# Order of the mixing in a hybrid decoder layer: memory queries behind the memory keys, the values of dilated group 0 between the two dilated pairs, values read per head

## The chip, the cores and the metric

The kernel runs on one core of one Trainium2 chip. The metric is the device time of one execution in microseconds, the median over several runs. TensorE does the matrix products, VectorE (DVE) and ScalarE (ACT) the elementwise work, GpSimd (POOL) a few small operations and its own DMA queue, and SyncE (SP) issues most DMAs. Each engine and each queue takes its instructions in a fixed order.

## The reference

One decoder layer on 512 tokens of width 1024: a SwiGLU half-step, a token mixing, a second SwiGLU half-step, each between two RMS norms. The change lies in the mixing, which has three branches:

- HGRN2, a chunked gated linear recurrence with four heads;
- a dilated sliding-window attention: three groups (window 128, 512, 2048 with dilation 1, 4, 16) of four heads of width 128, each head with its own queries, keys and values. The groups of a head are merged by their softmax maxima and sums;
- a cross-attention of four heads into 256 memory tokens.

```
def token_mixing(u, mem, ...):
    proj = u @ w_in
    hq, hf, hi, hog, dcols, mq, gl = jnp.split(proj, SPLITS, axis=-1)
    y_hg = rmsnorm(hgrn2(hq, hf, hi, lb), hg_norm_w) * sigmoid(hog)
    y_dil = dilated_attention(dcols)
    y_mem = memory_attention(mq, mem, mem_norm_w, w_mem_kv)
    y = gate0 * (y_hg @ w_br_hg) + gate1 * (y_dil @ w_br_dil) + gate2 * (y_mem @ w_br_mem)
    return y @ w_out
```

## The kernel before, in words

All products are float32 made of three float32r products of high and low parts. A weight tile is loaded by SP into a staging buffer (`st`, `sh`, `sum`), its high part is made on ACT and its low part on DVE (`split`, line 160), and the parts go to a pool of 18 buffers named `w`. Two column blocks of 128 are made together by seven half-width products (`pair`, line 366; weight sums on DVE in `wops`, line 285); one such pair is 84 matmuls of 128x256. Values, which need tokens on the partitions, are made by plain products of 128x512 (`values`, line 847).

Order of the work. `mixing` (line 910) runs over the tuple ORDER (line 42): hg0 and hg1 are the two pairs of recurrence heads, prep and kv normalise the memory and make its keys and values, v0, v1, v2 make the values of the three dilated groups, dil0 and dil1 the queries, keys and scores of two dilated heads each, mq0 and mq1 the memory queries of two heads each; b_hg, b_mem and b_dil are gates and output products of the branches.

The long tails of each head are generators. They are put between the matmuls by a planner: every matmul adds its planned time to a clock (`tick`, line 109), and a generator that yields a number of microseconds (the table LAT, line 47) is taken up again when that much has been planned. A framework then places the instructions in the streams of the engines, and may put an instruction that it holds to be ready ahead of an earlier one; the order in each stream is fixed when the program is built. Weight loads run ahead of their use as far as staging buffers are free.

- `mem_attention` (line 570): scores of a head into PSUM (line 579), maximum (581), exponential (585), normalisation (589), transposes (595), product with the memory values (602), copy (604).
- `dil_scores` (line 721): scores of one group of a head, to `s0` (group 0) or `s12` (groups 1 and 2).
- `dil_values` (line 744): maxima (748), exponentials (759), the statistics of the two kinds of tile exchanged through DRAM by four DMAs of POOL (764 to 769), a wait of LAT dil1 = 17, factors and scaling (771 to 785), a wait of dil2 = 5, and then for `s0` and after it for `s12`: eight transposes (795; seven for `s0`), evictions to SBUF (798, 800), a wait of dil3 = 3, products with the values (812), and the result copied to y (814) or added to it (817).
- `put_values` (line 863) writes the values of a group to DRAM on ACT's queue; `get_values` (line 870) reads them for two heads in the token order of the group by two DMAs of SP, 256 KB each in runs of 1 KB. `dil_pair` (line 920) calls it once per group, right behind the scores of that group.

PSUM has three buffers `px` for the tails, SBUF 37 buffers `slot` for everything of 128x512.

Of the kernel before, what the change touches and what calls it, by code (L numbers as in the profile page):

```python
# [12 lines left out]
ALU = mybir.AluOpType  # L13
# [4 lines left out]
P = 128  # L18
# [20 lines left out]
NST = 4  # L39
HT = T // 2  # L40

ORDER = ("hg0", "prep", "v1", "hg1", "v2", "kv", "v0", "dil0", "mq0", "mq1", "dil1", "b_hg", "b_mem", "b_dil")

CHUNKS1 = (2, 4, 4, 4, 4, 4)
CHUNKS2 = (2, 4, 4, 4, 4, 4)
# [1 line left out]
LAT = dict(comb=1.0, mem0=0.5, mem1=8.0, mem2=1.5, hg=1.5, hgx=6.0, hg1=6.0, hg2=11.0, hg3=6.0, hg4=6.0, dil0=4.0, dil1=17.0, dil2=5.0,  # L47
           dil3=3.0, norm=8.0, mnorm=5.0, mload=10.0, start=0.1, step=2.0, keep=2.0)
# [4 lines left out]
class Layer:  # L53
# [687 lines left out]
            for i in range(2):  # L741
                self.tt(s[i][:, :, g - 1, :], sp[:, 2 * i:2 * i + 2, :], nb, ALU.add)

    def dil_values(self, hd, s0, s12, st0, st1, v, out):
        nc = self.nc
        hs = slice((hd % 2) * P, (hd % 2) * P + P)
        for i in range(2):
            nc.vector.tensor_reduce(out=st1[:, 2 * i:2 * i + 2, 0:1], in_=s12[i].rearrange("p a g b -> p a (g b)"), axis=AX.X, op=ALU.max)

        def block(s, i):  # L750
            b = s[i // 2][:, i % 2, :, :].rearrange("p a b -> p (a b)")
            return b[:, P:] if (s is s0 and i == 0) else b

        for s, st in ((s0, st0), (s12, st1)):
            nm = self.sm(4, "nm")
            nc.vector.tensor_scalar(out=nm, in0=st[:, :, 0], scalar1=-SCALE, scalar2=None, op0=ALU.mult)
            for i in range(4):
                b = block(s, i)
                nc.scalar.activation(b, b, AF.Exp, bias=nm[:, i:i + 1], scale=SCALE, accum_out=st[:, i, 1:2])


        x0 = self.dram.tile([T, 2], F32, tag=f"x0_{hd}", name=f"x0_{hd}")
        x1 = self.dram.tile([T, 2], F32, tag=f"x1_{hd}", name=f"x1_{hd}")
        nc.gpsimd.dma_start(out=x0.rearrange("(j p) c -> p j c", p=P), in_=st0)
        nc.gpsimd.dma_start(out=x1.rearrange("(p a) c -> p a c", a=4), in_=st1)
        ot0 = self.small.tile([P, 4, 2], F32, tag="ot0", name=f"ot0_{hd}")
        ot1 = self.small.tile([P, 4, 2], F32, tag="ot1", name=f"ot1_{hd}")
        nc.gpsimd.dma_start(out=ot0, in_=x1.rearrange("(j p) c -> p j c", p=P))
        nc.gpsimd.dma_start(out=ot1, in_=x0.rearrange("(p a) c -> p a c", a=4))
        yield LAT['dil1']  # L770
        for s, own, oth in ((s0, st0, ot0), (s12, st1, ot1)):
            mm, c = self.sm(4, "mm"), self.sm(4, "c")
            wt = self.small.tile([P, 2, 4], F32, tag="wt", name=f"wt{self.uid()}")
            self.tt(mm, own[:, :, 0], oth[:, :, 0], ALU.max)
            self.tt(wt[:, 0, :], own[:, :, 0], mm, ALU.subtract)
            self.tt(wt[:, 1, :], oth[:, :, 0], mm, ALU.subtract)
            nc.scalar.activation(wt, wt, AF.Exp, scale=SCALE)
            self.tt(mm, wt[:, 0, :], own[:, :, 1], ALU.mult)
            self.tt(c, wt[:, 1, :], oth[:, :, 1], ALU.mult)
            self.tt(mm, mm, c, ALU.add)  # L780
            nc.vector.reciprocal(mm, mm)
            self.tt(c, mm, wt[:, 0, :], ALU.mult)
            for i in range(4):
                b = block(s, i)
                nc.vector.tensor_scalar(out=b, in0=b, scalar1=c[:, i:i + 1], scalar2=None, op0=ALU.mult)
        yield LAT['dil2']

        y = self.slot()
        for s in (s0, s12):
            pTs = []  # L790
            for i in range(2):
                tp = self.paux((P, 4, P))
                lo = 1 if (s is s0 and i == 0) else 0
                for j in range(lo, 4):
                    self.transpose(tp[:, j, :], s[i][:, j // 2, j % 2, :])
                pT = self.slot((P, 4, P))
                if s is s0:
                    nc.scalar.copy(pT[:, lo:, :], tp[:, lo:, :])
                else:
                    nc.vector.tensor_copy(out=pT, in_=tp)  # L800
                pTs.append(pT)
            yield LAT['dil3']
            po = self.paux((P, 4, P))
            for b in range(4):
                pT, j = pTs[b // 2], 2 * (b % 2)
                if s is s0:
                    pairs = [(v[0][b - 1], pT[:, j, :])] if b > 0 else []
                    pairs.append((v[0][b], pT[:, j + 1, :]))
                else:
                    pairs = [(v[1][b], pT[:, j, :]), (v[2][b], pT[:, j + 1, :])]  # L810
                for n, (vv, pp) in enumerate(pairs):
                    self.mm(po[:, b, :], vv[:, hs], pp, n == 0, n == len(pairs) - 1)
            if s is s0:
                nc.scalar.copy(y, po.rearrange("p a b -> p (a b)"))
            else:
                yv = y.rearrange("p (s a) -> p s a", a=4)
                self.tt(yv, yv, po.rearrange("p a s -> p s a"), ALU.add)
        out[hd] = y


# [46 lines left out]
            self.nc.scalar.dma_start(out=d[t * P:(t + 1) * P, :], in_=v[t][:, 0, :])  # L867
        return d

    def get_values(self, d, g, hp):  # L870

        rows = d.rearrange("(p a) c -> p a c", a=4) if g else d.rearrange("(j p) c -> p j c", p=P)
        out = []
        for i in range(2):
            r = self.slot((P, 2, 256))
            self.nc.sync.dma_start(out=r, in_=rows[:, 2 * i:2 * i + 2, hp * 256:hp * 256 + 256])
            out += [r[:, j, :] for j in range(2)]
        return out

    def branch(self, b, y, w_in, w_br, z, last):  # L880

# [28 lines left out]
    def mixing(self, a, ready, nbias):  # L910
        nc = self.nc
        w_in = a["w_in"][0]
        y_hg, y_mem, y_dil = [None] * H, [None] * H, [None] * H
        t_hg, t_mem, t_dil = [], [], []
# [3 lines left out]
            t_hg.append(self.spawn(self.hgrn(hp, f, q, o, vh, y_hg)))  # L918

        def dil_pair(hp):  # L920
            heads, v = [], [None] * 3
            for i in range(2):
                hd = 2 * hp + i
                nb = self.slot()
                self.fetch(nb, nbias[:, hd, :])
                s0 = [self.slot((P, 2, 2, P)) for _ in range(2)]
                s12 = [self.slot((P, 2, 2, P)) for _ in range(2)]
                st0 = self.small.tile([P, 4, 2], F32, tag="st0", name=f"st0_{hd}")
                st1 = self.small.tile([P, 4, 2], F32, tag="st1", name=f"st1_{hd}")
                heads.append((hd, nb, s0, s12, st0, st1))  # L930
            scores = [[], []]
            pairs = self.pairs([(w_in, c, c + 512) for c in (C_DIL + g * 1536 + (2 * hp + i) * P for g in range(3) for i in range(2))])
            for g in range(3):
                for i, (hd, nb, s0, s12, st0, st1) in enumerate(heads):
                    if g == 0:
                        q, k = self.project2(next(pairs))
                    else:
                        q, k = self.slot((P, 4, P)), self.slot((P, 4, P))
                        perm = lambda x: x.rearrange("p (s a) -> p a s", a=4)
                        views = lambda x: [(x[:, :, h * 64:(h + 1) * 64], perm) for h in range(2)]  # L940
                        self.pair_out(self.pair(next(pairs)), views(q), views(k))
                    scores[i].append(self.spawn(self.dil_scores(nb, g, q, k, s0 if g == 0 else s12, st0)))
                v[g] = self.get_values(vd[g], g, hp)
            for i, (hd, nb, s0, s12, st0, st1) in enumerate(heads):
                self.need(*scores[i])
                t_dil.append(self.spawn(self.dil_values(hd, s0, s12, st0, st1, v, y_dil)))

        vh = [x[:, 0, :] for x in self.values(w_in, C_HI, 512, ready)]
        self.reset = self.slot()
# [2 lines left out]
        z, vd = None, {}  # L952
        for n, step in enumerate(ORDER):
            if step in ("hg0", "hg1"):
                hgrn_pair(int(step[2]))
            elif step in ("v0", "v1", "v2"):
                g = int(step[1])
# [3 lines left out]
            elif step == "prep":  # L961
                mT = [(self.slot((P, 2, NMEM), F32R), self.slot((P, 2, NMEM), F32R)) for _ in range(4)]
                prep = self.spawn(self.mem_prep(a["mem"][0], a["mem_norm_w"][0], mT))
# [3 lines left out]
            elif step in ("mq0", "mq1"):  # L967
                hp = int(step[2])
                mq = self.pairs([(w_in, C_MQ + hp * 2 * P, C_MQ + hp * 2 * P + P)])
                for i, q in enumerate(self.project2(next(mq))):  # L970
                    hd = 2 * hp + i
                    t_mem.append(self.spawn(self.mem_attention(hd, q, mkT[hd], mv, y_mem)))
            else:
                b, y, tasks, w = {"b_hg": (0, y_hg, t_hg, "w_br_hg"), "b_mem": (2, y_mem, t_mem, "w_br_mem"), "b_dil": (1, y_dil, t_dil, "w_br_dil")}[step]
                self.need(*tasks)
                z = self.branch(b, y, w_in, a[w][0], z, n == len(ORDER) - 1)
        return z
# [140 lines left out]
```

## Time and profile before

| what | us |
|---|---|
| median of 3 runs | 1367.01 |
| lowest and highest of them | 1365.49 and 1369.76 |
| the profiled execution | 1367.62 |
| its span, first to last instruction | 1365.8 |
| TensorE busy in that span | 1331.6 |

Granted TensorE clock, mean over the span: 0.998. A line of the profile names the source line (L158 is line 158), the engine, the operation, the tiles written and read (out<-in), the shapes and the count. L158 is the helper `tt` (any DVE operation of two tensors), L161 the high part of a split, L341 to L343 the products of 128x512, L361 to L363 those of a pair, L348 the small products of the tails, L352 a transpose, L151 a weight load. An idle time names what ended it. Ends of matmuls are modelled, so the starts are what is read.

### The profile page before, as it was taken

Reading aid. Unit: us, or ns where it says so; the run is one execution under the profiler, and the core shown is the slowest. Engines: PE = TensorE matmul, PEld = TensorE weight load, DVE = VectorE, ACT = ScalarE, POOL = GpSimd, SP = SyncE. Lnnn points to the kernel's source line nnn. Section 1 sums busy time; section 2 is a strip of 40 time slices with the busy share of each in tenths; the row PEclk is TensorE's granted clock in tenths of the full one; section 3 lists DMA queues with packets and bytes.
Section 4 is the critical chain, followed back from the end, with each engine's and each line's share of the span. In section 5 each row is a group of like instructions: output and inputs, shape, how many; then the busy total and the mean of one; then the engine's idle time right before and its main releaser. Section 6 shows DMA issues by size and latency. Waiting matters only on the chain.

```text
span 1365.8 us, 24324 instructions
## 1 busy us (share of the span) xinstructions
PE 1331.6 (97%) x9197; PEld 1233.0 (90%) x9197; DVE 1050.7 (77%) x1996; ACT 742.2 (54%) x1527; POOL 107.0 (8%) x140
## 2 busy tenths in 40 slices
PE   6999999999999999999999999999999999999997
PEld 6999999999789888899899999999889999999996
DVE  6887776777798975598888988897478877677765
ACT  6665544555467655355554755566366655445541
POOL 1111111110100000000000100000011111111100
PEclk9999999999999999999999999999999999999999
DMA  9676565554435335334224333335465765655513
GB/s 271 141 182 184 148 156 142 143 151 125 168 94 177 96 98 163 123 102 117 63 78 124 100 95 93 108 94 154 135 190 135 186 181 151 152 139 148 146 47 139
DMA packets 238123, 185.76 MB, mean 136 GB/s; under 512 B 9109, under 2 KB 198966, under 8 KB 238006
## 3 DMA queue, kind: packets, MB, share of 16 engines
q1 hardware_dynamic: 224246, 160.02, 39.5%
q0 software_dynamic: 12032, 21.04, 9.4%
q10 hardware_dynamic: 1728, 3.15, 0.6%
q8 instruction: 72, 1.18, 0.3%
q14 instruction: 45, 0.37, 0.1%
HBM read 153.73 MB, written 9.47 MB: 119 GB/s over the span
## 4 chain that ended last, share of the span: by engine, by line
PE 87%; DVE 6%; issue 3%; DMA 2%; ACT 1%; POOL 1%; SPq 0%; POOLq 0%; DVEq 0%; ACTq 0%
PE ps L361 17%; PE ps L363 17%; PE ps L362 17%; PE ps L341 6%; PE ps L342 6%; PE ps L343 6%; PE px L341 5%; PE px L342 5%; PE px L343 5%; PE px L348 4%; DVE s L158 2%; PE px L352 1%; DVE w L158 1%; POOL r L181 1%; DVE s L244 1%
## 5 line engine op out<-in xcount | busy, mean ns | idle before, releaser
L161 ACT ACTIVATE w<-sum 128x512 fp32r<-128x512 f32 x288 | 180.2, 631 | 215.9 <-PE ps L362 180.3
L158 DVE TENSOR_TENSOR w<-sum,w 128x512 fp32r<-128x512 f32 x288 | 196.9, 687 | 76.9 <-ACT w L161 75.9
L361 PE MATMUL ps<-xhi,w 128*128 128x256 f32 x864 | 246.3, 285 | 0.9 <-ACT s L379 0.9
L363 PE MATMUL ps<-xhi,w 128*128 128x256 f32 x864 | 244.8, 283 | 0.0
L362 PE MATMUL ps<-xlo,w 128*128 128x256 f32 x864 | 244.4, 283 | 0.0
L161 ACT ACTIVATE w<-st 128x512 fp32r<-128x512 f32 x260 | 162.9, 630 | 126.7 <-PE ps L362 90.0
L158 DVE TENSOR_TENSOR w<-st,w 128x512 fp32r<-128x512 f32 x260 | 177.2, 688 | 39.3 <-ACT w L161 37.9
L158 DVE TENSOR_TENSOR s<-s,s 128x256 f32<-128x256 f32 (+3 forms) x316 | 176.8, 564 | 16.2 <-ACT s L161 4.6
L361 PEld LDWEIGHTS ps<-xhi,w 128*128 128x128 f32 x864 | 165.6, 192 | 3.8 <-ACT s L379 1.2
L362 PEld LDWEIGHTS ps<-xlo,w 128*128 128x128 f32 x864 | 165.6, 192 | 2.4 <-issue 0.2
L363 PEld LDWEIGHTS ps<-xhi,w 128*128 128x128 f32 x864 | 165.5, 192 | 0.0
L158 DVE TENSOR_TENSOR sum<-sum,st 128x512 f32<-128x512 f32 x176 | 120.4, 687 | 10.9 <-issue 5.0
L158 DVE TENSOR_TENSOR s<-s,ps 128x256 f32<-128x256 f32 (+1 forms) x194 | 92.3, 476 | 29.4 <-PE ps L343 24.0
L341 PE MATMUL px<-s,s 128*128 128x512 f32 x288 | 112.6, 391 | 0.0
L342 PE MATMUL px<-s,s 128*128 128x512 f32 x288 | 112.5, 391 | 0.0
L343 PE MATMUL px<-s,s 128*128 128x512 f32 x288 | 112.0, 389 | 0.0
L361 PE MATMUL ps<-t4hi,w 128*128 128x256 f32 x288 | 81.9, 284 | 0.8 <-ACT s L382 0.8
L361 PE MATMUL ps<-t3hi,w 128*128 128x256 f32 x288 | 82.6, 287 | 0.0
L362 PE MATMUL ps<-t3lo,w 128*128 128x256 f32 x288 | 82.0, 285 | 0.0
L361 PE MATMUL ps<-t1hi,w 128*128 128x256 f32 x288 | 81.7, 284 | 0.0
L363 PE MATMUL ps<-t1hi,w 128*128 128x256 f32 x288 | 81.6, 283 | 0.0
L362 PE MATMUL ps<-t2lo,w 128*128 128x256 f32 x288 | 81.5, 283 | 0.0
(186 smaller groups left out, 3344.2 us busy)
## 6 DMA issues: line engine op xcount, KB each, us to landing
st<-in_ffn_w_gu_dram SPq DMA_DIRECT2D x48, 512.0 KB, 4.9
st<-in_w_in_dram SPq DMA_DIRECT2D x48, 512.0 KB, 3.7
st<-in_ffn_w_down_dram SPq DMA_DIRECT2D x44, 512.0 KB, 3.8
sum<-in_ffn_w_gu_dram SPq DMA_DIRECT2D x80, 256.0 KB, 3.4
sh<-in_ffn_w_gu_dram SPq DMA_DIRECT2D x40, 256.0 KB, 3.8
sum<-sh POOLq DMA_DIRECT2D x40, 256.0 KB, 3.6
sum<-st POOLq DMA_DIRECT2D x40, 256.0 KB, 3.3
sum<-in_w_in_dram SPq DMA_DIRECT2D x32, 256.0 KB, 2.9
```

What stands on the lines that cost most here:

```text
L158: self.pin(self.nc.vector.tensor_tensor(out=out, in0=a, in1=b, op=op))
L161: self.pin(self.nc.scalar.activation(hi, src, AF.Copy))
L181: self.nc.gpsimd.tensor_tensor(out=r, in0=v, in1=self.mhalf[:, :1], op=ALU.pow)
L244: self.nc.vector.scalar_tensor_tensor(out=h[hf][:, cs], in0=y[hf][:, cs], scalar=r, in1=h[hf][:, cs], op0=ALU.mult, op1=ALU.add)
L341: mm(out, lhsT=lhs[0], rhs=rhs[0], start=first, stop=False)
L342: mm(out, lhsT=lhs[0], rhs=rhs[1], start=False, stop=False)
L343: mm(out, lhsT=lhs[1], rhs=rhs[0], start=False, stop=last)
L348: self.nc.tensor.matmul(out, lhsT=lhsT, rhs=rhs, start=start, stop=stop, **k)
L352: self.nc.tensor.transpose(out, in_, self.ident)
L361: mm(out, lhsT=lh, rhs=rh, start=first and k == 0, stop=False, skip_group_check=True)
L362: mm(out, lhsT=lh, rhs=rl, start=False, stop=False, skip_group_check=True)
L363: mm(out, lhsT=ll, rhs=rh, start=False, stop=k == 3, skip_group_check=True)
```

## The change

ORDER is rewritten: kv, mq0 and mq1 follow hg1, then come v2, dil0, v0, dil1. `get_values` reads one head by one DMA of 256 KB in runs of 512 bytes, and is called in `dil_values` itself: for groups 1 and 2 when the head's transposes are due, for group 0 when `s12` is transposed and the values of group 0 exist. `s12` is done before `s0`; y is written by ACT from the product of `s12` and the product of `s0` is added by DVE.

```diff
--- before.py
+++ after.py
@@ -39,7 +39,7 @@
 NST = 4
 HT = T // 2
 
-ORDER = ("hg0", "prep", "v1", "hg1", "v2", "kv", "v0", "dil0", "mq0", "mq1", "dil1", "b_hg", "b_mem", "b_dil")
+ORDER = ("hg0", "prep", "v1", "hg1", "kv", "mq0", "mq1", "v2", "dil0", "v0", "dil1", "b_hg", "b_mem", "b_dil")
 
 CHUNKS1 = (2, 4, 4, 4, 4, 4)
 CHUNKS2 = (2, 4, 4, 4, 4, 4)
@@ -741,9 +741,9 @@
             for i in range(2):
                 self.tt(s[i][:, :, g - 1, :], sp[:, 2 * i:2 * i + 2, :], nb, ALU.add)
 
-    def dil_values(self, hd, s0, s12, st0, st1, v, out):
-        nc = self.nc
-        hs = slice((hd % 2) * P, (hd % 2) * P + P)
+    def dil_values(self, hd, s0, s12, st0, st1, vd, out):
+
+        nc = self.nc
         for i in range(2):
             nc.vector.tensor_reduce(out=st1[:, 2 * i:2 * i + 2, 0:1], in_=s12[i].rearrange("p a g b -> p a (g b)"), axis=AX.X, op=ALU.max)
 
@@ -786,7 +786,9 @@
         yield LAT['dil2']
 
         y = self.slot()
-        for s in (s0, s12):
+        yv = y.rearrange("p (s a) -> p s a", a=4)
+        v = {g: self.get_values(vd[g], g, hd) for g in (1, 2)}
+        for s in (s12, s0):
             pTs = []
             for i in range(2):
                 tp = self.paux((P, 4, P))
@@ -799,6 +801,10 @@
                 else:
                     nc.vector.tensor_copy(out=pT, in_=tp)
                 pTs.append(pT)
+            if s is s12:
+                while 0 not in vd:
+                    yield LAT['dil3']
+                v[0] = self.get_values(vd[0], 0, hd)
             yield LAT['dil3']
             po = self.paux((P, 4, P))
             for b in range(4):
@@ -809,12 +815,11 @@
                 else:
                     pairs = [(v[1][b], pT[:, j, :]), (v[2][b], pT[:, j + 1, :])]
                 for n, (vv, pp) in enumerate(pairs):
-                    self.mm(po[:, b, :], vv[:, hs], pp, n == 0, n == len(pairs) - 1)
+                    self.mm(po[:, b, :], vv, pp, n == 0, n == len(pairs) - 1)
             if s is s0:
-                nc.scalar.copy(y, po.rearrange("p a b -> p (a b)"))
+                self.tt(y, y, po.rearrange("p a b -> p (a b)"), ALU.add)
             else:
-                yv = y.rearrange("p (s a) -> p s a", a=4)
-                self.tt(yv, yv, po.rearrange("p a s -> p s a"), ALU.add)
+                nc.scalar.copy(yv, po.rearrange("p a s -> p s a"))
         out[hd] = y
 
 
@@ -867,15 +872,12 @@
             self.nc.scalar.dma_start(out=d[t * P:(t + 1) * P, :], in_=v[t][:, 0, :])
         return d
 
-    def get_values(self, d, g, hp):
+    def get_values(self, d, g, hd):
 
         rows = d.rearrange("(p a) c -> p a c", a=4) if g else d.rearrange("(j p) c -> p j c", p=P)
-        out = []
-        for i in range(2):
-            r = self.slot((P, 2, 256))
-            self.nc.sync.dma_start(out=r, in_=rows[:, 2 * i:2 * i + 2, hp * 256:hp * 256 + 256])
-            out += [r[:, j, :] for j in range(2)]
-        return out
+        r = self.slot((P, 4, P))
+        self.nc.sync.dma_start(out=r, in_=rows[:, :, hd * P:hd * P + P])
+        return [r[:, j, :] for j in range(4)]
 
     def branch(self, b, y, w_in, w_br, z, last):
 
@@ -918,7 +920,7 @@
             t_hg.append(self.spawn(self.hgrn(hp, f, q, o, vh, y_hg)))
 
         def dil_pair(hp):
-            heads, v = [], [None] * 3
+            heads = []
             for i in range(2):
                 hd = 2 * hp + i
                 nb = self.slot()
@@ -940,10 +942,9 @@
                         views = lambda x: [(x[:, :, h * 64:(h + 1) * 64], perm) for h in range(2)]
                         self.pair_out(self.pair(next(pairs)), views(q), views(k))
                     scores[i].append(self.spawn(self.dil_scores(nb, g, q, k, s0 if g == 0 else s12, st0)))
-                v[g] = self.get_values(vd[g], g, hp)
             for i, (hd, nb, s0, s12, st0, st1) in enumerate(heads):
                 self.need(*scores[i])
-                t_dil.append(self.spawn(self.dil_values(hd, s0, s12, st0, st1, v, y_dil)))
+                t_dil.append(self.spawn(self.dil_values(hd, s0, s12, st0, st1, vd, y_dil)))
 
         vh = [x[:, 0, :] for x in self.values(w_in, C_HI, 512, ready)]
         self.reset = self.slot()
```

## Rows read from the trace of the kernel before

**Rows 1.** The page, part 1: busy us, share and instructions of each engine.
```profile
PE 1331.6 (97%) x9197; PEld 1233.0 (90%) x9197; DVE 1050.7 (77%) x1996; ACT 742.2 (54%) x1527; POOL 107.0 (8%) x140
```

**Rows 2.** TensorE's waits, 380 to 870 us: waiter, releaser, total us, times, longest.
```profile
PE px L348 <- DVE s L158: 2.2, 3, 1.0
PE ps L342 <- DVE w L158: 1.8, 1, 1.8
PE px L348 <- ACT s L585: 1.6, 1, 1.6
PE px L352 <- DVE s L190: 1.0, 1, 1.0
PE ps L341 <- ACT w L161: 0.7, 1, 0.7
```

**Rows 3.** TensorE's timeline: start us, us, what, xcount, idle before and its releaser.
```profile
642.95 1.13 PE L348 MATMUL px<-s,s 128*128 128x128 f32 x8 [0.95 <-DVE s L158]
...
656.23 2.20 PE L348 MATMUL px<-s,s 128*128 128x256 f32 x8 [1.02 <-DVE s L158]
...
660.42 1.13 PE L348 MATMUL px<-s,s 128*128 128x256 f32 x4 [1.64 <-ACT s L585]
...
769.85 0.50 PE L341 MATMUL ps<-s,w 128*128 128x512 f32 x1 [0.72 <-ACT w L161]
```

**Rows 4.** Stretches: length; busy PE, PEld, DVE, ACT, POOL; clock; DMA share; GB/s.
```profile
517.00:546.00 29.00, 29.00 (x200) 25.55 (x199) 14.91 (x28) 13.16 (x24) 1.88 (x2) 1.00 0.54 172
546.00:574.00 28.00, 28.00 (x150) 22.59 (x149) 14.03 (x26) 8.12 (x14) 0.00 (x0) 1.00 0.35 108
...
633.00:653.00 20.00, 19.05 (x160) 18.88 (x159) 13.43 (x34) 11.80 (x38) 3.17 (x5) 1.00 0.30 81
653.00:686.00 33.00, 30.34 (x218) 26.50 (x217) 31.98 (x98) 17.50 (x47) 0.76 (x1) 1.00 0.20 57
686.00:746.00 60.00, 59.90 (x455) 56.44 (x454) 51.84 (x113) 32.27 (x78) 1.31 (x2) 1.00 0.40 106
```

**Rows 5.** Timeline of VectorE and of ScalarE behind dil0.
```profile
652.42 0.23 DVE L158 TENSOR_TENSOR mm<-st,ot 128x4 f32<-128x4 f32 x2 [4.76 <-DMA ot<-x]
...
659.35 0.47 ACT L585 ACTIVATE s<-px,mnm 128x256 f32<-128x256 f32 x1 [4.28 <-DVE mnm L582]
```

**Rows 6.** Memory attention on VectorE by line: ns min/median/max, first and last start.
```profile
L581 DVE TENSOR_REDUCE mmx<-px x8: 690/692/692, 658.3 to 691.3; 128x2 f32<-128x512 f32 x8
...
L589 DVE TENSOR_SCALAR s<-s,ml x16: 345/348/351, 662.2 to 696.1; 128x256 f32<-128x256 f32 x16
...
L604 DVE COPY s<-px x4: 684/688/694, 669.9 to 702.5; 128x512 f32<-128x512 f32 x4
```

**Rows 7.** Softmax exponentials of the dilated heads on ScalarE, line 759.
```profile
L759 ACT ACTIVATE s<-s,nm x32: 387/494/514, 593.0 to 768.2; 128x256 f32<-128x256 f32 x28, 128x128 f32<-128x128 f32 x4
```

**Rows 8.** Value reads, line 876: issues on SP, and issue to landing.
```profile
L876 SPq DMA_DIRECT2D s<-v x12: 408/460/1092, 596.0 to 757.7; - x12
...
DMA to landing us min/median/max: 3.8/5.7/7.5
```

**Rows 9.** Tile sh, 256 KB weight loads, issue to landing.
```profile
DMA to landing us min/median/max: 2.7/3.5/7.3
```

**Rows 10.** SP's waits, 560 to 800 us: waiter, releaser, total us, times, longest.
```profile
SPq L151 <- DVE w L158: 147.0, 33, 17.4
...
SPq L876 <- PE ps L362: 0.9, 2, 0.5
```

**Rows 11.** Eight transposes on TensorE, and two copies of the dilated heads by line.
```profile
676.16 1.04 PE L352 MATMUL px<-ident,s 128*128 128x128 f32 x8
...
L800 DVE COPY s<-px x8: 681/682/685, 677.2 to 796.8; 128x512 f32<-128x512 f32 x8
...
L814 ACT COPY s<-px x4: 586/586/587, 676.4 to 795.3; 128x512 f32<-128x512 f32 x4
```

**Rows 12.** Value writes, line 867 on ACT's queue: issue to landing.
```profile
DMA to landing us min/median/max: 2.0/2.0/2.7
```

## The prediction

> **What bounds the kernel now.** I read the share of each engine first: TensorE is busy for 1331.6 of 1365.8 us [rows 1], so the order of its work can only be worth the time in which it stands still. Next come its waits in the mixing [rows 2]. Leaving out 1.8 us, which precede the mixing, they make 2.2 + 1.6 + 1.0 + 0.7 = 5.5 us. This is the ceiling of what a new order can give back, 0.4% of the time. 0.3% is about what a measurement of this kernel can tell from no change, and is 4.1 us: below 1362.9 or above 1371.1.
>
> The timeline places the waits [rows 3]. At 642.95 the last scores of dil0 wait 0.95 us for the keys that DVE writes. At 656.23 and 660.42 the first scores of the memory queries wait 1.02 us for DVE, and 1.64 us until ACT's exponentials free a PSUM buffer. At 769.85 the first weight of b_hg comes 0.72 us late from ACT. The 1.0 us on L190 in [rows 2] belongs to the normalisation of the memory, which stays where it is; the remaining 0.20 us of the 2.2 is dil1's last scores.
>
> Why the memory queries wait is seen on the other engines. DVE has stood for 4.76 us before the statistics of the dilated heads, which come by DMA [rows 5], with everything else on its queue behind them. Then it owes two things at once, the dilated tails and the memory tails: from 653 to 686 us it is busy for 31.98 of 33.00 us [rows 4]. ACT, with the exponentials of the memory heads, waits 4.28 us for DVE's maxima [rows 5], and with that TensorE.
>
> **The change, part by part.** The sum starts from the profiled execution, 1367.62 us, which lies 0.61 above the median of the runs, 1367.01.
>
> *Memory queries behind kv.* Nothing is added: the same two pairs, scores, exponentials and transposes are issued earlier. Their DVE work is 8 maxima of 0.692, 16 scalings of 0.348 and 4 copies of 0.688 us [rows 6], together 5.5 + 5.6 + 2.8 = 13.9 us. It leaves a stretch where DVE had 1.02 us free and goes to one behind kv, where DVE is busy for 14.91 of 29.00 us, and under v2, which now follows (for v0, the same product, DVE is busy for 14.03 of 28.00) [rows 4]. The wait for the statistics is no longer ahead of it. Both waits should go: -1.02 - 1.64 = **-2.66 us**. The other bound is that they come back in the new place, where the tail of hg1 uses the same three PSUM buffers: 0. I take the whole gain, since DVE enters the new place without a backlog. The queries' weight loads pass those of v2, v0 and dil0 on SP's queue, and kv's follow hg1's directly; POOL's queue only loses distance to dil0's statistics. I cost that at 0: TensorE waits for no load in [rows 2], and loads run ahead. If that cover is gone, a late load costs TensorE up to its landing time, 3.5 us [rows 9].
>
> *v0 between the dilated pairs.* Its plain products now follow dil0, and need weights split on ACT and DVE while ACT has the exponentials of two heads, 16 of 0.494 us [rows 7], or 7.9 us. The nearest row is the end of dil1, where b_hg's plain products follow the same exponentials and TensorE waits 0.72 us for ACT [rows 3]. Bounds: 0, if the weights were split before, and 0.72. I take **+0.72 us**. The 4.76 us in which DVE waits for the statistics now fall into v0, whose 28 us need only 14.03 of DVE [rows 4]: 0. The writes of v0 stand behind the exponentials on ACT's queue, and land 2.0 us after their issue [rows 12]; who waits for them is the read of group 0, and behind that, on SP's queue, the weight loads of dil1. A read before waited 0.9 us in all on that queue [rows 10]; bounds 0 and 2.0, and I take 0, since loads run ahead of their use and TensorE waits for none in [rows 2]. The 0.95 us at dil0's end stays: the same scores are forced out at the end of the pair, behind the same keys.
>
> *Values read per head when due.* The count stays 12 reads of 256 KB, each taking some 0.46 us of SP to issue [rows 8], in runs half as long. Their place changes: before, they were issued behind each group's scores and landed long before use; now they are issued when the transposes are due. Between issue and use lie eight transposes, which end 1.04 us after their start, and the planned 3 us of other products, so 4.0 us, with two evictions of 0.682 us beside them [rows 11]. A read took 3.8 to 7.5 us to land, 5.7 in the median [rows 8]. Weight loads of the same size, whose runs are 128 columns or 512 bytes as the new reads' are, landed in 3.5 us [rows 9]. So a head waits between 0 and 7.5 - 4.0 = 3.5 us; four heads, 0 to 14.0. I take **0**, the value of the loads with the same shape.
>
> The trace so shows no penalty for runs of 512 bytes against 1 KB: 3.5 us against 5.7 [rows 8, 9]. The Trainium skill, Perfetto Trace Analysis, section DMA Optimizations, speaks against this part: it has small DMAs, under 2 KB, carry significant overhead each, and would batch them. If halving the run doubled the landing to an estimated 11.4 us, the four heads would wait 4 x 7.4 us, and the time would be near 1395. The rows do not bear that out.
>
> *The swap of `s12` and `s0`.* ACT still makes four copies, of 0.586 us [rows 11], DVE four additions; the reordered write is now ACT's. Cost 0, far off TensorE's path; if the copy became slow it would hold a PSUM buffer a little longer. The buffers in SBUF are less used, since the values of a pair no longer wait through its scores: no cost, and no wait for one shows today beyond the 0.9 us.
>
> Sum: 1367.62 - 2.66 + 0.72 = 1365.68 for an execution like the profiled one, and with 0.61 off, **1365.1** as a median.
>
> **The rivals.**
>
> *A, the forecast*, chance 0.45: 1365.1, its own range 1363.4 to 1367.0 (with v0's weights on time 1364.4).
>
> *B, the wait only moves*, 0.13. The order in the tuple is not that of the streams, and hg1's tail takes PSUM and DVE as the dilated tails did. The 2.66 us stay and 0.72 is added: 1367.7. Against it: both new stretches have some 14 us of DVE free [rows 4].
>
> *C, the other waits go too*, 0.20. v0's products, ready early, fill the wait at dil0's end, and the relief of DVE reaches dil1's: 1367.01 - 2.66 - 0.95 - 0.72 - 0.20 = 1362.5. For it: those are DVE and ACT waits [rows 3]; against: the keys are forced out as before.
>
> *D, TensorE waits for the values*, 0.22, the slower one. TensorE takes its stream in order, so a product placed too soon after its read holds all pairs behind it. At the median landing each head is short by 5.7 - 4.0 = 1.7 us; four heads give 6.8, and 1371.9. At 7.5 us it is 14.0, and 1379.1. It decides from 6.0 us in all, 1.5 per head. For it: SP is mostly waiting, 147.0 us of 240 for buffers that DVE frees, up to 17.4 at once [rows 10], and a read placed behind such a load is late with it. Against: two heads run together and share a wait, and the framework may put pair products ahead. The Trainium skill's rule on small DMAs, cited above, would raise this price to 4 x 7.4 us; as the rows stand I leave it 0.02 of the 0.22.
>
> **How the numbers follow.** The likeliest is A, 1365.1. Faster by over 0.3% is nearly all of C: 0.20. Slower is D with a little of B: 0.23. A and B make the rest, 0.57. The range runs from 1361.8, a little below C, to 1372.5, which takes in D at the median landing; D's upper part and a luckier C are left out, less than 2 in 10.
>
> **What would show it.** Right: TensorE's waits name neither L585 nor a memory score, DVE between kv and v2 is busier than [rows 4] but not full, and a wait on ACT stands at v0's first product. D shows as small products idle until a DMA of the value tiles. B shows as the same wait on L585 near 530 us. If TensorE's idle time grows in dil1's first pair by DVE's weight splits, the transition v0 to dil1 was costed too low, and the prediction is wrong there.

## The result, and the profile after

The changed kernel is slower: 1372.58 us median (13 runs, 1369.45 to 1376.12) against 1367.85 for the kernel before (13 runs on the same chip, 1365.36 to 1369.76), ratio 1.0031 with a 95% interval of 1.0020 to 1.0043. The forecast, 1365.1, has the wrong sign, and the median lies 0.08 us above the end of the range. The profiled execution took 1375.53 us, span 1373.8.

Part 1 of its page, busy time by engine, answers to [rows 1]:

```profile
PE 1337.2 (97%) x9197; PEld 1239.0 (90%) x9197; DVE 1049.6 (76%) x1996; ACT 742.3 (54%) x1527; POOL 106.7 (8%) x140
```

The count of TensorE's instructions is the same, 9197, and yet it is busy for 5.6 us more. Its waits from 380 to 870 us, to be read against [rows 2]:

```profile
PE px L348 <- DMA s<-v: 3.1, 1, 3.1
PE px L348 <- DVE st L734: 2.2, 2, 1.9
PE ps L342 <- DVE w L158: 1.8, 1, 1.8
PE px L352 <- DVE s L190: 1.0, 1, 1.0
PE ps L341 <- ACT w L161: 0.7, 1, 0.7
PE px L348 <- DVE s L158: 0.7, 2, 0.5
```

The wait of 1.64 us on the exponentials, L585, is gone, and that on L158 fell from 2.2 to 0.7 us: the memory queries no longer hold TensorE. Two waits are new, one on DVE's masking of scores (L734) and one on a read of values. TensorE's timeline places them, and the wait of b_hg that stood at 769.85 in [rows 3]:

```profile
610.83 0.70 PE L348 MATMUL px<-s,s 128*128 128x256 f32 x2 [1.88 <-DVE st L734]
...
695.05 0.77 PE L348 MATMUL px<-s,s 128*128 128x128 f32 x2 [3.10 <-DMA s<-v]
...
777.70 0.50 PE L341 MATMUL ps<-s,w 128*128 128x512 f32 x1 [0.72 <-ACT w L161]
```

The first stands at the first scores of dil0, the second in the first pair of dil1. Stretches behind the two, with the columns of [rows 4] (length; busy PE, PEld, DVE, ACT, POOL; clock; DMA share; GB/s):

```profile
608.00:611.00 3.00, 1.12 (x6) 0.67 (x6) 2.97 (x8) 1.23 (x3) 0.00 (x0) 1.00 0.31 87
611.00:614.00 3.00, 3.00 (x17) 2.95 (x18) 2.44 (x10) 1.01 (x3) 0.00 (x0) 0.64 0.50 126
614.00:617.00 3.00, 3.00 (x22) 3.00 (x22) 2.12 (x5) 2.21 (x9) 0.00 (x0) 0.80 0.15 54
...
692.00:694.00 2.00, 0.00 (x0) 0.00 (x0) 1.89 (x4) 0.00 (x0) 0.00 (x0) 0.93 1.10 331
694.00:697.00 3.00, 1.95 (x9) 1.98 (x10) 0.41 (x1) 0.00 (x0) 0.00 (x0) 0.50 0.57 163
697.00:700.00 3.00, 3.00 (x16) 3.00 (x16) 1.57 (x3) 0.09 (x1) 0.00 (x0) 0.50 1.02 287
700.00:703.00 3.00, 3.00 (x27) 3.00 (x26) 0.00 (x0) 1.98 (x4) 0.00 (x0) 0.91 0.09 28
```

The eighth column is the one that matters. Behind each wait the granted clock falls, to 0.50, which is 1.2 of 2.4 GHz (behind the first it is 0.50 from 612 to 615 us, within the two stretches shown); in [rows 4] it is 1.00 in every stretch. While TensorE works at that clock it loses, by length times what is missing from 1.00, 3.00 x 0.36 + 3.00 x 0.20 = 1.7 us behind the first wait, and from 695.05 to 703 us 4.95 x 0.50 + 3.00 x 0.09 = 2.7 us behind the second. So in this execution the wait of 1.88 costs 3.6 us, and that of 3.10 costs 5.8.

That accounts for this execution. What left: 1.02 + 1.64 of the queries, and 0.4 of the 0.95 at dil0's end (the wait on L158 has now 0.5 as its longest), 3.1 us. What came: 3.6 + 5.8 = 9.4. The balance is +6.3 us. By the timelines, from the first product of hg0 to the first of b_hg, the kernel before took 769.85 - 398.07 = 371.8 us and this one 777.70 - 399.77 = 377.9: +6.1. The rest of the 7.9 us between the two profiled executions lies ahead of the mixing, where the change is not (a clock of 0.52 from 383 to 386 us, behind a wait of 1.8 us that both kernels have); it comes and goes between executions.

These prices hold for the profiled execution, which is the second longest of the 13. Its mean granted clock is 0.994. That of the three longest, 1375.35 to 1376.12 us, is 0.993 or 0.994; that of the other ten, 1369.45 to 1373.20 us, is 0.995 to 0.998, and the kernel before had 0.998 in its profiled execution. So most executions seem to pay less for the clock than this one, and the medians are only 4.7 us apart. How the 4.7 us divide between waits and clock is not shown.

**Why the values came late.** SP's timeline, its issues around 690 us:

```profile
683.07 0.37 SPq L151 DMA_DIRECT2D sum<-in_w_in_dram  x1
685.60 0.37 SPq L151 DMA_DIRECT2D st<-in_w_in_dram  x1
686.06 1.01 SPq L141 DMA_DIRECT2D s<-in_nbias_dram  x2
687.12 1.33 SPq L879 DMA_DIRECT2D s<-v  x2
688.54 0.62 SPq L151 DMA_DIRECT2D sh<-in_w_in_dram  x1
694.37 2.30 SPq L879 DMA_DIRECT2D s<-v  x4
```

SP's waits from 660 to 700 us (as [rows 10]), and the landing time of the two reads issued at 687.12 (as [rows 8]):

```profile
SPq L151 <- DVE w L158: 27.4, 4, 13.8
SPq L879 <- DMA v<-s: 5.0, 1, 5.0
```

```profile
DMA to landing us min/median/max: 7.8/7.9/7.9
```

One weight load had held SP for 13.8 us, until DVE had split earlier weights. Then dil1's weights, two masks (L141), the reads of groups 1 and 2 and v0's last write all fell within 6 us, and the DMA engines moved 331 GB/s from 692 to 694 us. The reads took 7.8 us to land; TensorE was ready for them at 695.05 - 3.10 = 691.95, 4.8 us after their issue. 7.8 - 4.8 = 3.0 is the wait. Four more reads follow from 694.37. The first of them is a read of group 0, which held SP's queue for 5.0 us until v0's last write had landed; ACT had issued that write at 687.25, into the same burst, and it took 7 us.

**Why dil0 starts late.** DVE's timeline before the first scores:

```profile
588.87 2.00 DVE L158 TENSOR_TENSOR w<-sum,w 128x512 fp32r<-128x512 f32 x3 [0.46 <-ACT w L161]
...
600.86 0.69 DVE L158 TENSOR_TENSOR sum<-sum,sh 128x512 f32<-128x512 f32 x1 [2.51 <-issue]
```

The weight sum at 600.86 waits 2.51 us. The view names nobody for that wait ("issue"), but the semaphore events of the same trace do: it ends with the landing, at 600.78, of a load to `sh`. SP's issues around it:

```profile
592.10 0.37 SPq L151 DMA_DIRECT2D st<-in_w_in_dram  x1
592.56 1.01 SPq L141 DMA_DIRECT2D s<-in_nbias_dram  x2
594.51 0.38 SPq L151 DMA_DIRECT2D sh<-in_w_in_dram  x1
```

The load was issued at 594.51, behind another weight load and two masks, and landed 6.3 us later. It is a burst like that at v0's end, without the value reads. DVE then has no free time until the scores ask for it (2.97 of 3.00 us busy from 608 to 611), and they wait for L734.

### The profile page after: what moved, and what is told of

Same layout as the page of the kernel before. It is cut to its first block, busy times and chain, and to the rows that moved or that the text cites. A ratio compares the mean times of both kernels' runs of the same rounds, so it can differ in the third digit from the quotient of the medians.

```text
span 1373.8 us, 24321 instructions
## 1 busy us (share of the span) xinstructions
PE 1337.2 (97%) x9197; PEld 1239.0 (90%) x9197; DVE 1049.6 (76%) x1996; ACT 742.3 (54%) x1527; POOL 106.7 (8%) x140
## 4 chain that ended last, share of the span: by engine, by line
PE 84%; DVE 6%; issue 3%; DMA 3%; ACT 2%; POOL 1%; SPq 0%; DVEq 0%; POOLq 0%; ACTq 0%
PE ps L361 16%; PE ps L363 16%; PE ps L362 16%; PE ps L341 6%; PE ps L342 6%; PE ps L343 5%; PE px L341 5%; PE px L342 5%; PE px L343 5%; PE px L348 5%; DVE s L158 2%; PE px L352 1%; DVE w L158 1%; POOL r L181 1%; DVE s L244 1%
## 5 line engine op out<-in xcount | busy, mean ns | idle before, releaser
L158 DVE TENSOR_TENSOR w<-sum,w 128x512 fp32r<-128x512 f32 x288 | 196.7, 688 | 77.2 <-ACT w L161 76.2
L158 DVE TENSOR_TENSOR w<-st,w 128x512 fp32r<-128x512 f32 x260 | 178.0, 689 | 38.9 <-ACT w L161 31.8
L158 DVE TENSOR_TENSOR s<-s,s 128x256 f32<-128x256 f32 (+3 forms) x316 | 177.2, 565 | 16.0 <-ACT s L161 4.6
L158 DVE TENSOR_TENSOR sum<-sum,st 128x512 f32<-128x512 f32 x176 | 120.4, 688 | 13.8 <-issue 7.2
L158 DVE TENSOR_TENSOR s<-s,ps 128x256 f32<-128x256 f32 (+1 forms) x194 | 92.5, 477 | 29.2 <-PE ps L343 24.0
L363 PE MATMUL ps<-t1hi,w 128*128 128x256 f32 x288 | 82.2, 286 | 0.0
L362 PE MATMUL ps<-t1lo,w 128*128 128x256 f32 x288 | 81.9, 284 | 0.0
L361 PE MATMUL ps<-t2hi,w 128*128 128x256 f32 x288 | 81.8, 284 | 0.0
```

Source lines behind the costliest of these rows:

```text
L158: self.pin(self.nc.vector.tensor_tensor(out=out, in0=a, in1=b, op=op))
L361: mm(out, lhsT=lh, rhs=rh, start=first and k == 0, stop=False, skip_group_check=True)
L362: mm(out, lhsT=lh, rhs=rl, start=False, stop=False, skip_group_check=True)
L363: mm(out, lhsT=ll, rhs=rh, start=False, stop=k == 3, skip_group_check=True)
```

## The experiments

Theory: the queries' move is a gain, and what outweighs it is two late transfers (reads of values at v0's end, weights behind v2), each of which costs the wait and, in some executions, a fall of the clock behind it. Rivals: the late reads are slow in themselves; moving the queries is what costs; v0 between the pairs costs whatever the reads do. Each run stands against the kernel before on the same chip (medians 1367.00 in the first four runs, 1367.13 in the next four, 1367.26 in the last four).

### The parts alone

**e1_queries_only**: the kernel before, with the queries behind kv, and v2 and v0 ahead of dil0.

```diff
-ORDER = (..., "hg1", "v2", "kv", "v0", "dil0", "mq0", "mq1", "dil1", ...)
+ORDER = (..., "hg1", "kv", "mq0", "mq1", "v2", "v0", "dil0", "dil1", ...)
```

> The kernel before with kv, mq0 and mq1 behind hg1 and v2, v0, dil0, dil1 after them; the value reads stay as they were. Theory (three separate effects: the moved queries gain about 4 us, the late reads lose about 6, the start of dil0 behind v2 loses about 4): 1363 to 1365 us, no wait on L585, and dil0's first scores wait no longer than the 0.4 us they wait in the kernel before, since dil0 follows v0 as it did. Rival (the moved memory tails crowd VectorE and that is what delays dil0's first scores): the wait of 1.9 us on L734 comes back and the time is 1367 to 1369.

Measured: 1365.49 us, ratio 0.9987 (0.9977 to 0.9997). The wait on L585 is gone. The move is a gain of some 1.5 us, not a cost. It is less than the 2.66 that went; two small waits are new in its trace, 0.6 on L734 and 0.7 on L604 (DVE's copy of the product with the memory values). The time is 0.5 us above the theory's range, and well below the rival's.

**e2_reads_only**: the changed kernel in the order of the kernel before.

```diff
-ORDER = (..., "kv", "mq0", "mq1", "v2", "dil0", "v0", "dil1", ...)
+ORDER = (..., "v2", "kv", "v0", "dil0", "mq0", "mq1", "dil1", ...)
```

> The changed kernel with the order of before: only the late reads per head and the swap of s12 and s0 are left. Theory (the reads are late because SP was held and then sent a burst of weight loads, bias loads and reads at the end of v0): in the old order dil0's reads stand among the loads of mq0, without that burst; TensorE waits at most 1 us per pair for values and the time is 1367 to 1369. Rival (a read issued when due is late anywhere): a wait of 3 us and a fallen clock at each pair, 1373 to 1379.

Measured: 1365.50 us, 0.9991 (0.9982 to 0.9999). No wait names the values; the 1.6 us on L585 stay. Reads of one head in 512-byte runs, issued when due, cost nothing in themselves, nor does the swap of `s12` and `s0`. The time lies below the 1367 to 1369 of the theory.

**e4_v0_ahead**: the changed kernel with v0 back ahead of dil0.

```diff
-ORDER = (..., "v2", "dil0", "v0", "dil1", ...)
+ORDER = (..., "v2", "v0", "dil0", "dil1", ...)
```

> The changed kernel with v0 ahead of dil0 again, so that dil1 follows dil0 directly; late reads per head stay. Theory: no plain product stands between the pairs, SP isn't held by its weight buffers, and the reads wait for no write; the wait on s<-v falls to under 1 us: 1365 to 1368. Rival (the tails of dil0 need a light stretch of VectorE, which v0 gave): TensorE waits in dil1's first pair for weights or scores by 3 us or more, 1370 to 1373.

Measured: 1365.76 us, 0.9996 (0.9984 to 1.0007); no wait on a read, 0.7 us on L734. So each part is harmless without v0 between the pairs. With v0 there the reads are late, and the kernel is 0.3% slower, dil0's late start included.

### The reads of values in dil1's first pair

**e3_reads_early**: the reads of groups 1 and 2 at the start of the values of a head, 22 us of planned work earlier.

```diff
     def dil_values(self, hd, s0, s12, st0, st1, vd, out):
+        v = {g: self.get_values(vd[g], g, hd) for g in (1, 2)}
...
-        v = {g: self.get_values(vd[g], g, hd) for g in (1, 2)}
```

> The changed kernel with the reads of groups 1 and 2 issued at the start of dil_values, ahead of the softmax, some 22 us earlier. Theory (late reads cause the wait of 3.1 us at dil1's start, and the wait makes the clock fall): no wait on s<-v for these groups, granted clock 1.00 there, 1366 to 1368. Rival (the traffic at the end of v0 itself holds TensorE, through weights and the read of group 0): the wait moves to another tile and the time stays at 1371 to 1373.

Measured: 1368.25 us, 1.0013 (1.0001 to 1.0024). TensorE's waits from 380 to 870 us:

```profile
PE px L348 <- DVE st L734: 2.2, 2, 1.8
PE px L352 <- DVE s L190: 1.0, 1, 1.0
PE px L348 <- DVE s L158: 0.8, 2, 0.6
PE px L348 <- ACT s L800: 0.7, 1, 0.7
```

These are the four largest; the fifth is b_hg's 0.7. The wait for the values is gone, and with it the low clock: 1.00 from 691 to 700 us. In its place stand 0.7 us on ACT's copy of transposes (L800). At dil0's start all stays as it was (1.8 us on L734, a clock of 0.53 behind it).

**e10_reads_on_pool**: the reads on POOL's queue, past SP's held load.

```diff
-        self.nc.sync.dma_start(out=r, in_=rows[:, :, hd * P:hd * P + P])
+        self.nc.gpsimd.dma_start(out=r, in_=rows[:, :, hd * P:hd * P + P])
```

> The changed kernel with the value reads issued on GpSimd's queue instead of SP's. Theory (SP was held from 669 to 683 us by one weight load and the reads of groups 1 and 2 stood behind it and behind the bias loads): on the other queue they are issued earlier, some ms of the burst no longer precede them, and the wait for values falls to 1 us or less, 1366 to 1369. Rival (the reads are placed late by the plan, at the transposes): they leave at the same time and the wait stays above 2 us, 1371 to 1374.

Measured: 1376.47 us, 1.0076 (1.0055 to 1.0097), the slowest of all. POOL's timeline, and the wait that comes of it on TensorE's:

```profile
670.69 1.49 POOL L879 DMA_DIRECT2D s<-v  x2
691.22 2.99 POOL L879 DMA_DIRECT2D s<-v  x4 [19.03 <-DMA sum<-in_w_in_dram]
```

```profile
695.60 0.46 PE L348 MATMUL px<-s,s 128*128 128x128 f32 x2 [4.37 <-DMA s<-v]
```

Two reads now start 16 us earlier, and nobody waits for that head. But the other four stand 19 us on the queue and are issued only at 691.22. By the program the first of the four is group 0's, which needs v0's last write. The view names another DMA, but the semaphore events of the trace bear the program out: the queue went on at 690.54, when the last update of that write's semaphore had come at 690.52. ACT had issued the write at 684.11. The reads of groups 1 and 2 of the other head are among the four, and TensorE waits for them, longer than before; 1.9 us on DVE's copies (L802) are new as well. Neither the theory (1366 to 1369) nor the rival (1371 to 1374) foresaw the time. The Trainium skill, Perfetto Trace Analysis, section DMA Optimizations, suggests balancing DMAs across the engines that can issue them, where generating descriptors is the bottleneck. It was not the bottleneck here, where an issue takes SP some 0.6 us and one load had held it for 13.8, and the trace shows the other side: a queue of its own keeps its order too, and one read that is not ready holds all those behind it.

### dil0's start

**e8_bias_early**: all four mask biases are loaded at the start of kv, so that the bursts behind v2 and v0 are 512 KB smaller.

```diff
-                nb = self.slot()
-                self.fetch(nb, nbias[:, hd, :])
+                nb = nbs[hd]
...
             elif step == "kv":
                 self.need(prep)
+                for hd in range(H):
+                    nbs.append(self.slot())
+                    self.fetch(nbs[hd], nbias[:, hd, :])
```

> The changed kernel with the four bias loads of 256 KB (nbias) sent at the start of kv instead of at the head of each dilated pair, where two of them leave SP between the weight loads and the value reads. Theory (bursts: where a dilated pair follows plain products, SP is held by a weight buffer and then sends weights, biases and reads within 3 us, so that each lands late): dil0's wait on L734 falls from 1.9 to under 1 us, the wait for values at dil1's start from 3.1 to 1.5 us or less, the clock stays at 1.00 at one of the two places at least: 1366 to 1369. Rival (the reads and weights are late because they leave late, not because of what is ahead of them): both waits stay within 0.5 us, 1371 to 1373.

Measured: 1369.50 us, 1.0021 (1.0008 to 1.0034). DVE's wait before the weight sum fell from 2.51 to 1.26 us (the load to `sh` now lands in 5.0 us). Of TensorE's waits these bear on the theory:

```profile
PE px L348 <- DVE s L802: 2.1, 1, 2.1
...
PE px L348 <- DVE st L734: 0.6, 1, 0.6
PE px L348 <- DMA s<-v: 0.6, 1, 0.6
```

The clock stays 1.00 from 605 to 617 us. In dil1's first pair the reads land earlier, and what is late next is DVE's copy of the transposes (L802): 2.1 + 0.6 us instead of 3.1. The clock is 0.54 from 691 to 694 us. The time is 0.5 us above the theory's range.

**e9_v0_ahead_bias_early**: e8 with v0 ahead of dil0, as in e4.

> The changed kernel with v0 ahead of dil0 and the bias loads early. Theory (bursts): dil0's wait on L734, 0.7 us with v0 ahead alone, falls to the 0.03 us that it is in the kernel before; nothing else changes: 1363 to 1365, ratio to before 0.997 to 0.999. Rival (no burst effect there): the wait stays, the time is that of v0 ahead alone.

Measured: 1365.42 us, 0.9991 (0.9980 to 1.0002). The wait on L734 that e4 has is gone, but 1.7 us on L802 are new, behind b_hg's first product. The time is 0.4 us above the theory's range, and against e4 it is no difference that can be told.

**e6_dil0_behind_mq**: the changed kernel with v2 ahead of kv, so that dil0 follows the memory queries, which are pairs, and not a plain product.

```diff
-ORDER = (..., "hg1", "kv", "mq0", "mq1", "v2", "dil0", "v0", "dil1", ...)
+ORDER = (..., "hg1", "v2", "kv", "mq0", "mq1", "dil0", "v0", "dil1", ...)
```

> The changed kernel with the order hg0, prep, v1, hg1, v2, kv, mq0, mq1, dil0, v0, dil1: dil0 now follows a pair, not plain products; v0 stays between the dilated pairs. Theory (two separate costs, one at each place where a dilated pair follows plain products): the wait on L734 at dil0's start falls to 0.4 us or less and the clock stays at 1.00 there; the wait for values of some 3 us at dil1's start stays with its fall of the clock: 1368 to 1371. Rival (the memory tails crowd VectorE in dil0): they now run in dil0 itself, waits of 2 us or more in dil0 and 1372 or more.

Measured: 1371.00 us, 1.0030 (1.0018 to 1.0042). The wait on L734 is gone and the clock is 1.00 there; the wait for the values is still 2.7 us, with a clock of 0.72 from 691 to 697. The two losses are separate. The second alone is, in this profiled execution, 2.7 us of waiting and 6.00 x 0.28 = 1.7 us of clock, 4.4 in all; the next run takes it away from here.

### Both losses taken away, and v0 in other company

**e7_dil0_behind_mq_early**: e6 with the early reads of e3.

> The changed kernel with both of its losses taken away by order and place alone: v2 ahead of kv, so that dil0 follows the memory queries and not a plain product (run e6 showed no wait of 1.9 us at dil0's start that way), and the reads of groups 1 and 2 issued at the start of the values of a head (run e3 showed no wait for them that way). v0 stays between the dilated pairs. Theory (the loss is those two waits and the clock behind them, not v0's place as such): TensorE names neither s<-v nor L734 above 0.7 us, the granted clock is 1.00 from 600 to 760 us, and the time is 1365 to 1367. Rival 1 (v0 between the pairs costs by itself, whatever the reads): a wait of 1 us or more at dil1's start on DVE or ACT, and 1368 to 1370. Rival 2 (the reads of group 0, which must wait for v0's last write, become the wait): s<-v of 1 to 3 us near 690 us and 1369 to 1371.

Measured: 1366.11 us, 0.9996 (0.9987 to 1.0005), some 5 us under e6, whose ratio is 1.0030. All of TensorE's waits from 380 to 870 us:

```profile
PE ps L342 <- DVE w L158: 1.8, 1, 1.8
PE px L352 <- DVE s L190: 1.0, 1, 1.0
PE px L348 <- ACT s L585: 0.8, 2, 0.5
PE ps L341 <- ACT w L161: 0.7, 1, 0.7
PE px L348 <- DVE s L158: 0.7, 2, 0.5
```

No value, no L734, and a clock of 1.00 from 605 to 614 and from 685 to 697 us. Both rivals named for this run fall: v0 between the pairs costs nothing by itself that can be told here, and group 0's reads, though SP still stands for 3.5 us at v0's last write, hold nothing up.

**e11_reads_and_bias_early**: the changed kernel's own order, with the edits of e3 and e8.

> The changed kernel with its order, the reads of groups 1 and 2 at the start of the values of a head, and all four mask biases loaded at the start of kv. Alone the first gave 1368.25 and the second 1369.5 against 1367 before. Theory (the two losses are separate: the bias loads delay dil0's start, the late reads dil1's): the waits on L734 and s<-v are both under 0.7 us, the clock stays 1.00, and the time is 1365 to 1367. Rival (they are the same burst, in which one takes the place of the other): a wait of 1 to 2 us on DVE remains at dil1's start, as the 2.1 us on the additions of the values in the run with early biases, and the time is 1367.5 to 1369.

Measured: 1365.91 us, 0.9998 (0.9985 to 1.0010). No wait for a read, 0.7 us on L734, no copy late. The order of the change is then level with the kernel before; its 0.3% was late transfers. Between the changed kernel and e11 lie 4.5 us by the ratios and 6.1 by the medians, each against the kernel before on its chip; that is what the two delays cost on the whole, less than the 9.4 of the profiled execution.

**e13_v0_behind_old_queries**: late reads, v0 between the pairs, but the memory queries where they were before, between dil0 and v0.

```diff
-ORDER = (..., "hg1", "kv", "mq0", "mq1", "v2", "dil0", "v0", "dil1", ...)
+ORDER = (..., "hg1", "v2", "kv", "dil0", "mq0", "mq1", "v0", "dil1", ...)
```

> The part not yet run alone: the late reads and v0 between the dilated pairs, with v2 ahead of kv and the memory queries where they were, between dil0 and v0. The values of dil0's heads are then due under the queries, long before v0's end. Theory (the reads of groups 1 and 2 are late only because they fall due while SP is held by v0's weights): those reads land in time, and only the group 0 reads stand behind v0's last write; s<-v under 1 us, a wait on L585 of some 1.6 us as before, and 1366 to 1368. Rival (whatever is read behind v0's last write holds TensorE at dil1's start): s<-v of 2 to 4 us near 690 us, a stretch at a clock under 0.9 behind it, and 1370 to 1373.

Measured: 1364.37 us, 0.9978 (0.9968 to 0.9988), faster than the kernel before, and than the theory's 1366 to 1368. Against e6 (1.0030) only the place of the queries differs. Landing of the four reads of groups 1 and 2 of dil0's heads, issued from 643.4 to 645.4 us:

```profile
DMA to landing us min/median/max: 4.7/4.8/4.9
```

and the stretch over v0's end and dil1's start:

```profile
685.00:700.00 15.00, 15.00 (x130) 14.70 (x129) 9.62 (x18) 7.32 (x16) 0.00 (x0) 1.00 0.55 163
```

These reads fall due under the queries, not at v0's end. They land in 4.8 us instead of 7.8, and TensorE is busy for all of these 15 us. The wait on L585 is only 0.7 us: the queries in their old place hold TensorE less than before (why, was not tried). The late reads and v0 between the pairs are a good combination; what the change got wrong is that v0 follows dil0 at once, so that the 17 and 5 us which a head's values lag behind its scores run out just where v0 ends.

**e12_queries_bias_early**: e1 with the early biases of e8.

> The best run so far (queries behind kv, v2 and v0 ahead of dil0, reads as before: 1365.5) with all four mask biases loaded at the start of kv. Theory: the burst at the end of v0 gets 512 KB shorter, the wait of 0.6 us on L734 at dil0's start goes, and the time is 1364.5 to 1365.5, 0.998 to 0.999 of before. Rival (that wait is set by the weights, not by the biases): the 0.6 us stays and the time is 1365.5 to 1366.5.

Measured: 1363.84 us (8 runs), 0.9974 (0.9963 to 0.9984). Its waits:

```profile
PE ps L342 <- DVE w L158: 1.9, 2, 1.8
PE px L352 <- DVE s L190: 1.0, 1, 1.0
PE ps L341 <- ACT w L161: 0.7, 1, 0.7
PE px L348 <- DVE s L158: 0.4, 2, 0.2
```

The 0.6 us on L734 is gone as the theory had it, and the 0.7 us on L604 too; the time is 0.7 us below the theory's range. It has the lowest median of all, and like e13 it beats both kernels; the intervals of the two overlap.

## Why the prediction was wrong

**The queries behind kv: right in mechanism, too large in size.** -2.66 us was predicted; both waits went, and nothing came in their place behind kv. The kernel with only this move is faster, but by 1.5 us: 0.6 us on L734 and 0.7 on L604 came elsewhere. In the changed kernel DVE is busy for 43.55 of 47.00 us from 503 to 550 and for 18.00 of 28.00 from 546 to 574: fuller than the prediction argued from [rows 4], and still TensorE waits for nothing there.

**Values read per head when due: the step that failed.** The working was right: a landing less the time from issue to use, which was put at 4.0 us and measured 4.8. "I take 0, the value of the loads with the same shape" took the landing of a weight load, 3.5 us [rows 9], the median of loads from the whole execution. The reads of one head fell due when SP had just been let go: they took 7.8 us, beyond the 7.5 that was the upper end, and TensorE stood for 3.10 us where the sum had 0. The row that pointed there was cited, but under rival D: SP held for up to 17.4 us [rows 10], "and a read placed behind such a load is late with it". The rule of the Trainium skill on small DMAs (Perfetto Trace Analysis, DMA Optimizations) was rightly not taken: the twelve reads of 512-byte runs in the changed kernel landed in 4.6 us in the median, those of 1 KB before in 5.7 [rows 8], and e2 shows no wait for them.

**v0 between the dilated pairs: mis-sized both ways.** The +0.72 on ACT did not come. The write, bounded at 2.0 us, took 7 and held SP for 5.0; e7, where it still holds SP for 3.5, shows no wait of TensorE from it. And that v2 would now run straight into dil0 was in no term: 1.88 us at dil0's start.

**The clock: missing.** Every wait was priced at its length. In the profiled execution the two new ones cost 3.6 + 5.8 us for 5.0 of waiting. The clock's share of that, 1.7 + 2.7 = 4.4 us, is there by itself more than the bound of 0.3%; most of the 13 executions, with a higher mean clock, seem to pay less.

**The rivals.** D had the mechanism, TensorE held by a value read behind a held load, and gave 1371.9 at the median landing; but it reached that with four waits of 1.7 us, where the trace has one of 3.10, the clock, and dil0's start. It "decides from 6.0 us in all": the one wait with its clock made 5.8. The likeness of the times is luck, that of the mechanism is not. C fell: b_hg's 0.72 us stays in every run, though the 0.95 us at dil0's end, which the forecast had stay, fell to 0.5. A chance of 0.22 looks too low for D now, since the place of the reads, right behind a plain product and its held load, could be read from the diff and [rows 10].

What stays open: why SP's hold ahead of dil0 is 34.0 us in the changed kernel and 17.4 before. It is 34.0 in e1 as well, where the same masks stand in the burst behind it and the wait on L734 is only 0.6 us; so the length of the hold does not decide. Taking the masks out cuts the wait to 0.6 us in e8, but why e1 gets by with them was not tried.

## What to carry to other kernels

When a transfer is moved to "when due", find out what else its queue and the DMA engines owe at that moment: behind a load that waits for buffers, everything comes at once, and landing times from quieter moments don't hold. Look at when a delayed generator runs out against the end of the product above it; the same reads were free with the memory queries between dil0 and v0. A read that waits for a write belongs behind the reads that are ready, on whichever queue.

## What was not expected of the hardware

In the profiled execution of the changed kernel, single waits of 1.88 and 3.10 us, in a kernel that is otherwise dense, were followed by a granted clock of 0.50 (1.2 GHz): 0.64 and 0.80 in two stretches of 3 us behind the first, 0.50 in two behind the second. It does not always come. The wait of 1.8 us near 380 us, which all kernels have, was followed by 0.52 in the profiled execution of the changed kernel and by 1.00 in that of the kernel before; the waits of 1.02 and 1.64 us of the kernel before, and the 1.7 us on L802 in e9, were followed by 1.00 as well. 256 KB reads landed in 7.8 us in the burst that moved 331 GB/s from 692 to 694 us, and in 4.8 us in e13, under the queries.
